# The mixer's weight parts kept in DRAM from the first token block on

## The chip, the cores and the metric

The kernel runs on one core of one Trainium2 chip. The metric is device time in microseconds for one execution. TensorE (PE) multiplies matrices out of SBUF into PSUM; VectorE (DVE) and ScalarE (ACT) do elementwise work; GpSimd (POOL) does small elementwise work and issues some of the transfers; SyncE (SP) issues most of the transfers. Each engine takes its instructions strictly in the order in which the built program has them.

## The reference, cut to what matters

One decoder layer over 2048 tokens of width 1024, in float32. A state-space branch (512 wide) and a sliding-window attention branch (512 wide) are mixed, and a gated feed-forward part follows:

```
y_ssm = glu(gelu(ssm(u)) @ w_glu + b_glu)          # w_glu: 512 x 1024
y_attn = sliding_window_attention(q, k, v, sinks)
merged = concat(rms_norm(y_ssm, g_ssm_out), rms_norm(y_attn, g_attn_out))
h = h + rms_norm(merged @ w_out, g_post_mix)       # w_out: 1024 x 1024
h = h + rms_norm(swiglu(rms_norm(h, g_pre_ffn)), g_post_ffn)
```

The change concerns `w_glu` and `w_out`. All products keep close to float32 accuracy: each operand is split into a high part (what the matmul format fp32r holds) and a low part (the rest), and three matmuls are summed: high by high, high by low, low by high (`mm3`, L216).

## The kernel before

The program has three phases. `phase_proj` computes the projections and the state-space scan and leaves them in DRAM. `phase_mix` (L692) computes the attention, the gated state-space output and the output projection, from about 340 to 800 us of the span. `phase_ffn` is the feed-forward part, until the end.

`phase_mix` goes over four blocks of 512 tokens, here called blocks 0 to 3. `dense_stream` (L930) has for each block first a **glu stage**: 8 jobs, each with one 128x512 weight tile of `w_glu` and 12 matmuls into a bank `ps_z`; after each pair of jobs ACT takes the sigmoid (`sig`, L952), DVE forms `glu` (L954), both split it into `sh` and `sl`, ACT squares it (L963) and POOL adds the squares up in `sqs`. Then come 16 **out jobs** with tiles of `w_out` into four banks `ps_wo`: 8 with the attention's operands `mah` and `mal`, then 8 with `sh` and `sl`. The sums of squares go through a small matmul (`ps_sqs`, L985). The banks of `ps_z` and `ps_wo` are the same four, so an out job's bank is free only when `glu` has read the `ps_z` in it. The attention (`attn_stream`, L760) is woven in between; its difference tile `dv` is made by POOL (L848). The row work of the block before (`post_norm`, L1009: squares on ACT, `mixr` on DVE, residual rows `res_m` loaded on SP, `hd` stored by POOL) falls into the next glu stage, and so does `channel_steps` (L1104: `hx`, `hT`, `ho`, `hb`), which prepares the feed-forward operands.

The weights of all 4 x 24 = 96 jobs come through `weights` and `fill_weights` (L889 to L912): three jobs ahead of its use, a 256 KB tile `gwr` is loaded by SP, ACT rounds it to the high part `gwh` (L170, or L173 with a gain), and DVE forms the low part `gwl` (L171 or L174). Each of the three has four buffers in the pool `g_w`, so job j needs the `gwh` and `gwl` buffers that job j-4 has used. Blocks 1 to 3 load and split the same 24 tiles again, with the same result.

The order on each engine is set when the program is built: a scheduler places instructions by priority (weights have 300 steps of precedence, L891) and by when it thinks that buffers come free.

Of the kernel before, what the change touches and what calls it, by code (L numbers as in the profile page):

```python
# [9 lines left out]
F32 = mybir.dt.float32  # L10
# [9 lines left out]
P = 128  # L20
# [23 lines left out]
def f32(ap):  # L44
    return ap.bitcast(F32)


class Layer:
# [129 lines left out]
    def setup(self):  # L178
        ctx, tc, nc, I = self.ctx, self.tc, self.nc, self.I
# [13 lines left out]
        d = self.dr  # L193
# [6 lines left out]
        self.bT_d = [[d.tile([P, 4, TB], F32, name=f"bTd_{s}_{i}") for i in range(7)] for s in range(2)]  # L200
        self.fx_d = [[d.tile([2, 7, P, TB], F32, name=f"fxd_{s}_{jp}") for jp in range(NJP)] for s in range(2)]
        self.ws_d = [[d.tile([2, P, 512], F32, name=f"wsd_{i}_{jp}") for jp in range(NJP)] for i in range(4)]
        self.cos_d = d.tile([8, SEQ], F32, name="cosd")
        self.sin_d = d.tile([8, SEQ], F32, name="sind")
        self.nsin_d = d.tile([8, SEQ], F32, name="nsind")
# [691 lines left out]
    def fill_weights(self, last):  # L897
        nc, I, gw = self.nc, self.I, self.gw
        while len(self.got) <= last:
            job = self.jobs[len(self.got)]  # L900
            n = "_".join(str(x) for x in job)
            raw = gw.tile([P, 512], F32, tag="wr", name=f"gwr_{n}")
            wh = gw.tile([P, 512], F32R, tag="wh", name=f"gwh_{n}")
            wl = gw.tile([P, 512], F32R, tag="wl", name=f"gwl_{n}")
            if job[0] == "g":
                nc.sync.dma_start(raw, I["w_glu"][job[2]])
                self.split(wh, wl, raw)
            else:
                nc.sync.dma_start(raw, I["w_out"][job[2], :, job[3] * 512:(job[3] + 1) * 512])
                c = KD + job[2]  # L910
                self.split(wh, wl, raw, self.gain[:, c:c + 1] if job[2] > 3 else None)
            self.got.append((wh, wl))  # L912

    def y_tiles(self, b):
# [625 lines left out]
```

## Time and profile before

| | before |
|---|---|
| runs | 2172.40, 2168.85, 2166.42 us; median 2168.85 |
| the profiled execution | 2164.03 us, its span 2162.3 us |
| mean granted TensorE clock | 0.975 of full speed |
| busy in the span | PE 93%, PEld (weight loads) 75%, DVE 64%, ACT 43%, POOL 14% |
| DMA | 379.7 MB, mean 176 GB/s |

Times in the traces count from the start of the span. The tables by stretch give for each engine the busy time in us and, in brackets, its instructions; then the granted TensorE clock, the mean busy share of the 16 DMA engines, and the GB/s that they moved. A number in square brackets at the end of a row is idle time of that engine just before it, with what ended it.

### The profile page before, as it was taken

The numbers are of one execution on the slowest core, as the hardware profiler recorded it, in microseconds if no ns is written. First come the engines' busy times: TensorE is split into PE (matmuls) and PEld (weight loads), VectorE is DVE, ScalarE is ACT, GpSimd is POOL, SyncE is SP. The second block draws the span as 40 slices with busy tenths as digits, with TensorE's granted clock in tenths as the row PEclk, the third lists the DMA queues.
The fourth block names the chain that finished last, engine by engine and source line by source line (L and its number), as shares of the span: only waits on it lengthen the run. The fifth ranks groups of instructions, "written<-read, shape, count | busy, mean of one in ns | idle before, by whom it ended". The sixth has DMA issues, their size and how long they took to land.

```text
span 2162.3 us, 25813 instructions
## 1 busy us (share of the span) xinstructions
PE 2012.2 (93%) x9200; PEld 1631.6 (75%) x9200; DVE 1389.5 (64%) x2199; ACT 925.1 (43%) x1468; POOL 301.7 (14%) x655
## 2 busy tenths in 40 slices
PE   7998887999999797999989998999999999999996
PEld 5777665787878675878768876887788888888885
DVE  7876888887676748556455655446766555554446
ACT  6433114976566545333323334345333333334443
POOL 3211000112223322212122110001100000000001
PEclk9999998999899998999999999999999999999998
DMA  8566657534246745657666476666523222246665
GB/s 276 213 229 191 200 148 190 144 100 158 67 148 202 270 155 178 240 138 204 208 194 155 153 264 218 199 192 231 171 102 124 95 99 105 89 165 224 204 195 185
DMA packets 177425, 379.73 MB, mean 176 GB/s; under 512 B 32864, under 2 KB 53856, under 8 KB 177104
## 3 DMA queue, kind: packets, MB, share of 16 engines
q1 hardware_dynamic: 138112, 259.89, 38.1%
q0 software_dynamic: 32512, 109.79, 15.6%
q10 hardware_dynamic: 6672, 8.40, 1.3%
q8 instruction: 72, 1.18, 0.2%
q14 instruction: 57, 0.47, 0.1%
HBM read 281.87 MB, written 119.21 MB: 185 GB/s over the span
## 4 chain that ended last, share of the span: by engine, by line
PE 42%; issue 27%; DMA 10%; DVE 7%; POOL 4%; ACT 3%; SPq 0%; DVEq 0%; POOLq 0%; ACTq 0%
PE ps_dn L221 5%; PE ps_dn L219 5%; PE ps_dn L220 5%; PE ps_gb L219 2%; PE ps_gb L221 2%; PE ps_gb L220 2%; PE ps_wo L219 2%; PE ps_wo L221 2%; PE ps_wo L220 2%; DMA hx<-hd 1%; DMA hr<-bTd 1%; DMA tab<-tabd 1%; PE ps_O L871 1%; PE ps_O L870 1%; PE ps_gc L219 1%
## 5 line engine op out<-in xcount | busy, mean ns | idle before, releaser
L219 PE MATMUL ps_gb<-bh,wh 128*128 128x512 f32 x704 | 280.3, 399 | 17.6 <-ACT wh L170 8.3
L221 PE MATMUL ps_gb<-bh,wl 128*128 128x512 f32 x704 | 275.8, 394 | 3.8 <-DVE wl L171 3.7
L220 PE MATMUL ps_gb<-bl,wh 128*128 128x512 f32 x704 | 277.7, 394 | 0.3 <-DVE bl L171 0.2
L221 PE MATMUL ps_dn<-wh_d,wl_x 128*128 128x512 f32 x616 | 241.4, 393 | 7.5 <-DVE wl_x L171 5.5
L219 PE MATMUL ps_dn<-wh_d,wh_x 128*128 128x512 f32 x616 | 241.3, 392 | 6.1 <-ACT wh_x L170 3.2
L220 PE MATMUL ps_dn<-wl_d,wh_x 128*128 128x512 f32 x616 | 240.7, 391 | 0.0
L219 PEld LDWEIGHTS ps_gb<-bh,wh 128*128 128x128 f32 x704 | 133.4, 190 | 54.3 <-ACT wh L170 10.4
L221 PEld LDWEIGHTS ps_gb<-bh,wl 128*128 128x128 f32 x704 | 133.4, 189 | 34.5 <-DVE wl L171 4.9
L220 PEld LDWEIGHTS ps_gb<-bl,wh 128*128 128x128 f32 x704 | 133.5, 190 | 29.8 <-DVE bl L171 1.5
L219 PE MATMUL ps_gc<-bh,wh 128*128 128x512 f32 x352 | 138.6, 396 | 6.9 <-ACT bh L170 6.7
L221 PEld LDWEIGHTS ps_dn<-wh_d,wl_x 128*128 128x128 f32 x616 | 115.8, 189 | 36.3 <-DVE wl_x L171 9.2
L170 ACT CAST wh<-fr 128x1024 fp32r<-128x1024 f32 (+1 forms) x88 | 73.4, 835 | 158.5 <-issue 87.4
L219 PEld LDWEIGHTS ps_dn<-wh_d,wh_x 128*128 128x128 f32 x616 | 116.3, 189 | 31.7 <-ACT wh_x L1089 4.2
L220 PE MATMUL ps_gc<-bl,wh 128*128 128x512 f32 x352 | 138.8, 395 | 0.0
L221 PE MATMUL ps_gc<-bh,wl 128*128 128x512 f32 x352 | 138.6, 394 | 0.0
L171 DVE TENSOR_TENSOR wl_x<-xr,wh_x 128x1024 fp32r<-128x1024 f32 x72 | 81.6, 1133 | 88.8 <-ACT wh_x L170 88.8
L171 DVE TENSOR_TENSOR wl_d<-dr,wh_d 128x1024 fp32r<-128x1024 f32 x84 | 95.1, 1132 | 61.5 <-ACT wh_d L170 61.5
L220 PEld LDWEIGHTS ps_dn<-wl_d,wh_x 128*128 128x128 f32 x616 | 116.3, 189 | 24.1
L170 ACT CAST wh_x<-xr 128x1024 fp32r<-128x1024 f32 x72 | 70.7, 982 | 118.9 <-PE ps_dn L220 115.6
L170 ACT CAST wh_d<-dr 128x1024 fp32r<-128x1024 f32 x84 | 82.4, 981 | 89.2 <-PE ps_dn L220 64.1
L75 DVE TENSOR_TENSOR q<-ps_ga,q 128x512 f32<-128x512 f32 x44 | 30.4, 690 | 113.7 <-PE ps_ga L221 113.2
L171 DVE TENSOR_TENSOR wl<-sb,wh 128x1024 fp32r<-128x1024 f32 x44 | 53.8, 1223 | 67.2 <-ACT wh L170 67.2
(368 smaller groups left out, 4623.1 us busy)
## 6 DMA issues: line engine op xcount, KB each, us to landing
fr<-in_w_gu SPq DMA_DIRECT2D x88, 512.0 KB
xr<-fxd SPq DMA_DIRECT2D x70, 512.0 KB
dr<-wsd SPq DMA_DIRECT2D x40, 512.0 KB
fxd<-f POOLq DMA_DIRECT2D x22, 768.0 KB, 4.3
gwr_o<-in_w_out SPq DMA_DIRECT2D x64, 256.0 KB
wsd<-in_w_down POOLq DMA_DIRECT2D x30, 512.0 KB, 10.6
dr<-in_w_down SPq DMA_DIRECT2D x30, 512.0 KB
raw<-in_xT SPq DMA_DIRECT2D x56, 256.0 KB
```

Source lines behind the costliest of these rows:

```text
L75: (eng or self.nc.vector).tensor_tensor(out=out, in0=a, in1=b, op=op)
L170: nc.scalar.copy(hi, x)
L171: nc.vector.tensor_tensor(out=lo, in0=x, in1=f32(hi), op=ALU.subtract)
L219: t.matmul(out, wh, mh, start=first, stop=False, skip_group_check=more)
L220: t.matmul(out, wh, ml, start=False, stop=False, skip_group_check=more)
L221: t.matmul(out, wl, mh, start=False, stop=last, skip_group_check=more)
L870: nc.tensor.matmul(O[:, g, :], pts[v][1][:, g, :], self.V[:, i - 1, v, :], start=True, stop=False)
L871: nc.tensor.matmul(O[:, g, :], pts[v][0][:, g, :], dv[:, v, :], start=(i == 0), stop=True)
```

## The change

Block 0 (`job[1]` is the block) loads and splits as before and then stores both parts in DRAM, one DMA of 256 KB each, issued by POOL: 48 stores. Blocks 1 to 3 load the two parts straight into `gwh` and `gwl` with two DMAs of 256 KB on SP, and have neither the raw tile nor the split: 144 loads of parts in the place of 72 raw loads, and 72 fewer splits on ACT and on DVE.

```diff
+        self.gw_d = [[d.tile([P, 512], F32, name=f"gwd_{i}_{o}") for o in "hl"] for i in range(24)]
...
             n = "_".join(str(x) for x in job)
-            raw = gw.tile([P, 512], F32, tag="wr", name=f"gwr_{n}")
             wh = gw.tile([P, 512], F32R, tag="wh", name=f"gwh_{n}")
             wl = gw.tile([P, 512], F32R, tag="wl", name=f"gwl_{n}")
+            kept = self.gw_d[len(self.got) % 24]
+            if job[1]:
+                for t, k in zip((wh, wl), kept):
+                    nc.sync.dma_start(f32(t), k)
+                self.got.append((wh, wl))
+                continue
+            raw = gw.tile([P, 512], F32, tag="wr", name=f"gwr_{n}")
             if job[0] == "g":
                 nc.sync.dma_start(raw, I["w_glu"][job[2]])
                 self.split(wh, wl, raw)
...
                 self.split(wh, wl, raw, self.gain[:, c:c + 1] if job[2] > 3 else None)
+            for t, k in zip((wh, wl), kept):
+                nc.gpsimd.dma_start(k, f32(t))
             self.got.append((wh, wl))
```

Line numbers of the changed program are higher by 1 up to the function and by 9 behind it. SP's queue in the glu stage of block 1, before: the raw loads stand together, ahead of the residual rows `res_m`.

```order
L906 DMA gwr_g_1_6_4994<-in_w_glu 128x512
L906 DMA gwr_g_1_3_5040<-in_w_glu 128x512
L906 DMA gwr_g_1_7_5085<-in_w_glu 128x512
L909 DMA gwr_o_1_4_0_5173<-in_w_out 128x512
L909 DMA gwr_o_1_5_0_5221<-in_w_out 128x512
L909 DMA gwr_o_1_6_0_5269<-in_w_out 128x512
L1029 DMA res_m0_2_5078<-in_x 128x1024
L909 DMA gwr_o_1_7_0_5326<-in_w_out 128x512
L1029 DMA res_m0_3_5147<-in_x 128x1024
```

The same place of SP's queue now.

```order
L908 DMA gwh_g_1_3_5124<-gwd_6_h_165 128x512
L908 DMA gwl_g_1_3_5125<-gwd_6_l_166 128x512
L1038 DMA res_m0_2_5160<-in_x 128x1024
L908 DMA gwh_g_1_7_5167<-gwd_7_h_167 128x512
L908 DMA gwl_g_1_7_5168<-gwd_7_l_168 128x512
L1038 DMA res_m0_3_5227<-in_x 128x1024
L908 DMA gwh_o_1_4_0_5253<-gwd_8_h_169 128x512
L908 DMA gwl_o_1_4_0_5254<-gwd_8_l_170 128x512
L1038 DMA res_m1_0_6165<-in_x 128x1024
L908 DMA gwh_o_1_5_0_5299<-gwd_9_h_171 128x512
```

The two parts of one job now stand behind a residual row of 512 KB that was loaded after them before.

POOL's queue in block 0, before: the small adds of the attention (`dv`) and of the squares (`sqs`) follow one another.

```order
L630 DMA kd_2_93<-qe_2_4_3216 2x8x512
L75 TENSOR_TENSOR dv_3_3937<-Vres_159 128x130
L75 TENSOR_TENSOR dv_4_4067<-Vres_159 128x130
L75 TENSOR_TENSOR sqs_0_3388<-sqs_0_3388,sig_0_1_3685 128x512
L75 TENSOR_TENSOR sqs_0_3388<-sqs_0_3388,sig_0_2_3861 128x512
```

The same place of POOL's queue now, from the eighteenth store on.

```order
L920 DMA gwd_8_l_170<-gwl_o_0_4_0_3907 128x512
L920 DMA gwd_9_h_171<-gwh_o_0_5_0_3984 128x512
L75 TENSOR_TENSOR dv_3_4005<-Vres_207 128x130
L920 DMA gwd_9_l_172<-gwl_o_0_5_0_3985 128x512
L920 DMA gwd_10_h_173<-gwh_o_0_6_0_4077 128x512
L75 TENSOR_TENSOR dv_4_4137<-Vres_207 128x130
L75 TENSOR_TENSOR sqs_0_3436<-sqs_0_3436,sig_0_1_3747 128x512
L920 DMA gwd_11_h_175<-gwh_o_0_7_0_4236 128x512
```

Nineteen stores have come in front of `dv_3`, and `dv_4` stands behind the store of the high part of out job 6.

PE at the end of block 1's glu stage, before: the third and fourth bank (`ps_wo_559`, `ps_wo_560`) come late, and products of the next weight tiles are drawn forward.

```order
L221 MATMUL ps_wo_558_5323<-gwh_o_1_4_0_5174,mal_5_4483 128x512
L219 MATMUL ps_wo_557_5322<-gwh_o_1_5_0_5222,mah_4_4301 128x512
L220 MATMUL ps_wo_557_5322<-gwl_o_1_5_0_5223,mah_4_4301 128x512
L221 MATMUL ps_wo_557_5322<-gwh_o_1_5_0_5222,mal_4_4302 128x512
L219 MATMUL ps_wo_559_5324<-gwh_o_1_4_0_5174,mah_6_4834 128x512
```

The same place of PE's queue now.

```order
L222 MATMUL ps_wo_558_5397<-gwh_o_1_4_0_5253,mal_5_4567 128x512
L220 MATMUL ps_wo_559_5398<-gwh_o_1_4_0_5253,mah_6_4924 128x512
L221 MATMUL ps_wo_559_5398<-gwl_o_1_4_0_5254,mah_6_4924 128x512
L222 MATMUL ps_wo_559_5398<-gwh_o_1_4_0_5253,mal_6_4925 128x512
L220 MATMUL ps_wo_560_5399<-gwh_o_1_4_0_5253,mah_7_5156 128x512
```

The first weight tile is now used for all four banks before the second.

## Rows read from the trace of the kernel before

**Rows 1.** The page's first part, PE: busy us, share of the span, instructions.

```profile
PE 2012.2 (93%) x9200; PEld 1631.6 (75%) x9200; DVE 1389.5 (64%) x2199; ACT 925.1 (43%) x1468; POOL 301.7 (14%) x655
```

**Rows 2.** The table by stretch: from and to, length, then PE, PEld, DVE, ACT, POOL busy us with their instructions, granted clock, DMA share, GB/s.

```profile
515.00:525.00 10.00, 9.81 (x44) 7.80 (x43) 8.32 (x10) 5.43 (x10) 2.42 (x8) 1.00 0.40 117
525.00:535.00 10.00, 7.00 (x30) 5.12 (x28) 10.00 (x11) 8.69 (x15) 3.32 (x3) 1.00 0.94 352
535.00:545.00 10.00, 6.18 (x19) 4.66 (x19) 6.78 (x8) 5.99 (x9) 8.79 (x18) 0.83 0.87 264
545.00:555.00 10.00, 9.52 (x47) 9.52 (x47) 3.31 (x9) 1.96 (x5) 0.84 (x2) 0.54 0.12 29
555.00:565.00 10.00, 10.00 (x55) 9.06 (x56) 6.68 (x15) 4.81 (x11) 0.00 (x0) 0.77 0.26 80
...
640.00:650.00 10.00, 6.70 (x37) 5.16 (x36) 10.00 (x11) 8.92 (x13) 6.36 (x8) 1.00 0.97 339
...
710.00:720.00 10.00, 9.55 (x40) 7.52 (x39) 7.43 (x11) 3.33 (x4) 2.13 (x3) 0.84 0.98 343
720.00:730.00 10.00, 8.87 (x40) 7.03 (x39) 7.56 (x13) 6.05 (x10) 2.86 (x4) 1.00 0.98 336
...
760.00:770.00 10.00, 8.48 (x41) 6.66 (x40) 7.94 (x10) 7.95 (x13) 5.99 (x16) 1.00 0.99 373
```

**Rows 3.** PE's timeline in blocks 1 to 3, all rows from 524 to 800 us before which it waited more than 0.9 us except one at 648 us and one at 661 us, and the two rows that bound a pair of glu jobs: start us, us, engine, line, what, and the idle time before.

```profile
523.89 0.50 PE L219 MATMUL ps_z<-yh,gwh_g 128*128 128x512 f32 x1 [0.18 <-ACT sig L952]
...
529.50 0.39 PE L219 MATMUL ps_wo<-gwh_o,mah 128*128 128x512 f32 x1
...
531.89 0.50 PE L219 MATMUL ps_wo<-gwh_o,mah 128*128 128x512 f32 x1 [1.55 <-DVE glu L954]
535.38 0.60 PE L219 MATMUL ps_wo<-gwh_o,mah 128*128 128x512 f32 x1 [1.83 <-ACT sig L952]
545.48 0.38 PE L985 MATMUL ps_sqs<-ones,sqs 128*128 128x1 f32 x2 [3.92 <-POOL sqs L75]
...
643.39 0.50 PE L219 MATMUL ps_wo<-gwh_o,mah 128*128 128x512 f32 x1 [1.55 <-DVE glu L954]
...
708.18 0.79 PE L219 MATMUL ps_wo<-gwh_o,sh 128*128 128x512 f32 x1 [4.81 <-DVE mixr L997]
727.10 0.47 PE L219 MATMUL ps_z<-yh,gwh_g 128*128 128x512 f32 x1 [1.13 <-ACT wh L170]
733.81 1.97 PE L1125 MATMUL ps_hT<-ident,hx 128*128 128x128 f32 x8 [3.03 <-ACT hx L1117]
753.68 0.50 PE L219 MATMUL ps_wo<-gwh_o,mah 128*128 128x512 f32 x1 [0.92 <-DVE glu L954]
756.14 0.50 PE L219 MATMUL ps_wo<-gwh_o,mah 128*128 128x512 f32 x1 [1.48 <-ACT sig L952]
762.27 0.50 PE L219 MATMUL ps_wo<-gwh_o,mah 128*128 128x512 f32 x1 [1.52 <-DVE glu L954]
```

**Rows 4.** DVE's timeline around the end of block 1's glu stage, in the same columns.

```profile
524.54 0.74 DVE L174 SCALAR_TENSOR_TENSOR gwl_o<-gwr_o,c_gains,gwh_o 128x512 fp32r<-128x512 f32 x1
...
528.19 1.79 DVE L174 SCALAR_TENSOR_TENSOR gwl_o<-gwr_o,c_gains,gwh_o 128x512 fp32r<-128x512 f32 x1
...
531.10 0.74 DVE L954 SCALAR_TENSOR_TENSOR glu<-ps_z,l_b_glu,sig 128x512 f32<-128x512 f32 x1
531.76 0.74 DVE L174 SCALAR_TENSOR_TENSOR gwl_o<-gwr_o,c_gains,gwh_o 128x512 fp32r<-128x512 f32 x1
...
534.54 0.74 DVE L174 SCALAR_TENSOR_TENSOR gwl_o<-gwr_o,c_gains,gwh_o 128x512 fp32r<-128x512 f32 x1
...
537.84 0.74 DVE L954 SCALAR_TENSOR_TENSOR glu<-ps_z,l_b_glu,sig 128x512 f32<-128x512 f32 x1
```

**Rows 5.** The weight tiles by instruction over the whole span: line, engine, operation, what, count, then ns at least, in the median and at most, first and last start in us.

```profile
L909 SPq DMA_DIRECT2D gwr_o<-in_w_out x64: 327/328/570, 374.8 to 781.7; - x64
L173 ACT ACTIVATE gwh_o<-gwr_o,c_gains x32: 704/716/759, 384.2 to 768.9; 128x512 fp32r<-128x512 f32 x32
L174 DVE SCALAR_TENSOR_TENSOR gwl_o<-gwr_o,c_gains,gwh_o x32: 720/744/2125, 386.5 to 769.6; 128x512 fp32r<-128x512 f32 x32
L170 ACT CAST gwh_o<-gwr_o x32: 602/621/642, 448.5 to 791.2; 128x512 fp32r<-128x512 f32 x32
L171 DVE TENSOR_TENSOR gwl_o<-gwr_o,gwh_o x32: 680/692/693, 449.1 to 791.9; 128x512 fp32r<-128x512 f32 x32
...
L170 ACT CAST gwh_g<-gwr_g x32: 602/620/624, 352.5 to 741.0; 128x512 fp32r<-128x512 f32 x32
L171 DVE TENSOR_TENSOR gwl_g<-gwr_g,gwh_g x32: 680/690/694, 353.2 to 745.1; 128x512 fp32r<-128x512 f32 x32
```

**Rows 6.** Transfers: from the chain of work in order of time the time of one raw weight load (start us, us); from POOL's timeline the issue of a 512 KB store; and from the instructions on `mixr` between 500 and 560 us the time from issue to landing of four such stores.

```profile
344.31 3.75 DMA gwr_g<-in_w_glu
...
521.86 0.62 POOL L1033 DMA_DIRECT2D hd<-mixr  x1 [5.21 <-DVE mixr L75]
...
DMA to landing us min/median/max: 4.7/5.9/7.4
```

**Rows 7.** Block 0: a `dv` on POOL, and on DVE the first weight split behind it.

```profile
406.19 0.42 POOL L75 TENSOR_TENSOR dv<-Vres 128x130 f32<-128x130 f32 x1 [12.64 <-PE ps_O L871]
...
410.42 0.74 DVE L174 SCALAR_TENSOR_TENSOR gwl_o<-gwr_o,c_gains,gwh_o 128x512 fp32r<-128x512 f32 x1
```

## The prediction, made blind

> **What bounds the kernel now.** I read the page's first part, then the table by stretch, then TensorE's timeline for every wait in blocks 1 to 3, and last the weight tiles by instruction. PE is busy for 93% of the span, DVE for 64%, ACT for 43% [rows 1]. So work taken from DVE or ACT is worth only what PE waited for it, and what PE's clock lost behind such waits. The reader is to see in [rows 3] that these waits sit where a glu stage hands over to the out jobs, and in [rows 2] that DVE is there busy for 10.00 of 10 us (525 to 535, 640 to 650) while the DMA engines too are near their limit: a mean busy share of 0.94 to 0.99 at 336 to 373 GB/s. The change takes work from the first of these two resources and puts more on the second. That is the whole question.
>
> **What is removed.** Each of 72 jobs loses an ACT instruction of 0.62 or 0.72 us and a DVE instruction of 0.69 or 0.74 us [rows 5]: with the medians 24 glu jobs, 24 out jobs with a gain and 24 without give 47 us of ACT and 51 us of DVE. Most of it lies beside PE's work and is worth nothing there. It counts in these places.
>
> Block 1's change-over. PE waits 1.55 us for `glu`, 1.83 for `sig` and 3.92 at `ps_sqs` for the sum of squares that POOL forms from what `sig` and `glu` led to: 7.30 us [rows 3]. In that time DVE has no idle time, and four weight splits (0.74 + 1.79 + 0.74 + 0.74 = 4.0 us) stand before the last `glu` at 537.84 [rows 4]. Without them that `glu` starts about 4 us earlier; ACT's splits go as well. Of 7.30 us I leave about 2, for the residual rows' work, which stays: a gain of 5.3. At most all 7.3 go, at least nothing, if `glu` then waits for something else.
>
> The clock behind it. In the three stretches from 535 to 565 the granted clock is 0.83, 0.54 and 0.77, after 1.00 before the waits [rows 2], and PE is busy for 9.52 and 10.00 us in the last two, so the time there is the clock's. The loss is 10 x (0.17 + 0.46 + 0.23) = 8.6 us. The 0.54 is about the lower of the two levels, 1.2 of 2.4 GHz. If PE's gap shrinks from 7.3 to 2 us the clock may hold or may still fall; bounds 0 and 8.6, and I take the half, 4.3, since a wait of 1.55 us at 643 left the clock at 1.00 in its stretch, while one of 4.81 at 708 stands ahead of a stretch at 0.84 [rows 2, 3].
>
> Blocks 2 and 3. Block 2 has a wait of 1.55 us for `glu`; the share kept in block 1 (5.3 of 7.3, 0.73) gives 1.1. Block 3 has 0.92, 1.48 and 1.52 us for `glu` and `sig`, and 1.13 us directly for ACT's high part of a glu weight: 5.05 us in all, of which the same share is 3.7 [rows 3]. The waits for `mixr` (4.81) and `hx` (3.03) come from row work that stays: 0, at best the 4.81 too.
>
> **What is added to the transfers.** A job of blocks 1 to 3 now loads 512 KB instead of 256. Two glu jobs take 529.50 - 523.89 = 5.6 us on PE, one 2.8 [rows 3], so weights alone ask for 0.524 MB / 2.8 us = 187 GB/s where it was 94. Averaged over the span there is room. In the saturated stretches (525 to 535, 640 to 650, 710 to 730, 760 to 770 in [rows 2], 50 us) there is none. I count 14 jobs there, fewer than 50 / 2.8 = 18 because PE waits in them: 14 x 0.262 = 3.7 MB more, at 0.35 MB per us (their mean) 10.5 us. Loads are issued three jobs ahead, 3 x 2.8 = 8.4 us; of this a raw load of 3.75 us alone, and 4.7 to 7.4 us for a transfer of 512 KB among others [rows 6], leave about 4. So I let half of the 10.5 reach PE: a loss of 5.3, with bounds 0 and 10.5 from this term by bandwidth alone.
>
> The Trainium skill, "DMA: Bandwidth & Descriptors" (Measured; Where 436 GB/s comes from), gives 425 GB/s for a large read on one core whose neighbour is idle, and about 358 per core when both read. By the first the 3.7 MB would take 8.7 us and by the second 10.3 (an estimate from that page), so the loss would be 4.4 or 5.2 in the place of 5.3; the trace's fullest stretch has 373 GB/s at a share of 0.99 and so stands by the second.
>
> The queue. SP takes 0.33 us per issue [rows 5], and 144 issues replace 72, 24 us more in blocks 1 to 3: no limit by itself. But the raw tile gave the load four buffers of its own, free as soon as a split had read it; now a load may start only when PE has done with job j-4, and both loads of a job stand in line behind the residual rows, which wait for DVE's `mixr` adds. With four buffers the period of a job is max(11.2, L + 2.8) / 4 us, where L is the time from a buffer's freeing to the landing of both parts. L up to 8.4 us costs nothing. 512 KB landed in 4.7, 5.9 (median) and 7.4 us [rows 6], so it just fits; if SP is held for 2 us in addition, it does not. In the sum this is 0, and the price of the last rival.
>
> **Block 0's stores.** POOL issues 48 stores, 0.62 us each by a 512 KB store in its queue [rows 6]: 30 us of a POOL that is busy 14% [rows 1]. Nineteen come in front of `dv_3`, and `dv_4` stands behind one whose weight split is the row at 410.42, where a `dv` of the attention ran at 406.19 [rows 7]. So `dv` may be up to 4.2 us later, and who waits for it is the attention, not at once PE, which has products of out jobs beside it. I take 0; bounds 0 and 4. No stall of the buffers: four of them, and a store needs 4.7 to 7.4 us, about what two or three jobs take.
>
> **The sum**, against the profiled execution (2164.03 us: a span of 2162.3 and 1.7 around it): -5.3 - 4.3 - 1.1 - 3.7 + 5.3 + 0 + 0 = -9.1, so 2155. The median of the runs is 4.8 above that execution; for a median I forecast 2168.85 - 9.1 = 2160.
>
> **Rivals.** *The waits vanish wholly.* If the last `glu` no longer binds, 7.3 + 8.6 + 1.55 + 5.05 = 22.5 us go and some 2.5 come from DMA: -20, 2149. For it speaks that four splits are more than either single wait for `glu` or `sig`; against it the saturated transfers in the same stretches.
>
> *A transfer takes the place of the split.* PE then waits for weights where it waited for `glu`: -14.4 of gains and up to 10.5 + 2 of losses, -2, 2167. For it: DVE's busiest stretches are DMA's too [rows 2]. Against it: the first out jobs' weights come three jobs early.
>
> *Stores that cannot start.* If a POOL store could not be issued while DVE works, each of the 24 pairs would be held by half a DVE instruction or so, 24 x 0.35 = 8 us of later buffers in block 0, which use up the gain: -1, 2168. Against it: the issue of `hd` took 0.62 us, and four such stores landed within 7.4 us [rows 6], from stretches in which DVE was busy for 8.32 and 10.00 of 10 us [rows 2]. The Trainium skill, "SBUF — State Buffer" (SBUF: two separate sides), has such a rule: a DMA issued by GpSimd waits while DVE runs an operation that takes both of its ports.
>
> *Slower: weights late on SP.* Both parts stand in SP's order behind residual rows and `hx` work, with only four buffers. From L above 8.4 us each job loses (L - 8.4) / 4; with L = 10.4, that is a landing of 7.4 us and 3 us of SP waiting, 0.5 us on each of the 40 jobs that lie in or beside the row work of blocks 1 to 3 is +20, and the DVE and clock gain of about 10 stays: +10, 2179. For it: the order on SP, where a job's loads now stand behind a row of 512 KB that was loaded after them. Against it: the median landing of 5.9.
>
> **How the numbers follow.** Forecast 0.33 (own range 2154 to 2164), vanishing waits 0.17, transfer in their place 0.26, held stores 0.04, late weights 0.20. The extremes by the bounds are 7.3 + 8.6 + 1.55 + 5.05 + 4.81 = -27 (2142) and 10.5 + 4 = +15 without a gain (2184). The range of 8 in 10 is 2142 to 2182. A change of 0.3%, 6.5 us (2162.3 to 2175.4), is about what a measurement can tell from none. Faster: 0.33 x 0.85 + 0.17 + a little of the third, 0.46; same: the rest of these, the third and fourth, and a tenth of the last, 0.35; slower: 0.19.
>
> **What would show it.** Right: DVE busy below 9 in 525 to 535; no PE wait over 1 us at `ps_sqs` in block 1; a clock above 0.9 in most of 535 to 565; PE waits named for `gwh` or `gwl` loads under 0.5 us on average, with L under 8.4. Wrong: PE rows in blocks 1 to 3 ended by DMA of several us each, the more of them in the stretches with a DMA share over 0.95; or `dv` waits in block 0; or the same gap at `ps_sqs`, ended by another producer, with the same fall of the clock.

## The result, and the profile after

| | before | changed |
|---|---|---|
| first measurement, 4 runs each | median 2168.68 us | median 2179.49 us, ratio 1.0051, 95% interval 1.0031 to 1.0072 |
| second, 35 and 12 runs | median 2174.28 us | median 2179.81 us, ratio 1.0021, 95% interval 1.0001 to 1.0040 |
| the profiled execution (span) | 2162.3 us | 2176.2 us |
| mean granted TensorE clock | 0.975 | 0.969 |
| DMA | 379.7 MB | 411.2 MB |

The kernel is slower, by 0.2 to 0.5%; the lower end of the second interval all but touches no change. The page's first part of the changed kernel against [rows 1]: DVE has lost 47 us of work and ACT 41 (51 and 47 had been worked out), and PE, which does the same products, is busy for 10 us more.

```profile
PE 2022.5 (93%) x9200; PEld 1640.7 (75%) x9200; DVE 1342.6 (62%) x2127; ACT 883.9 (41%) x1396; POOL 318.5 (15%) x703
```

To find where, I cut PE's timeline at the first product of each block's glu stage and at the first of the feed-forward part. First the kernel before, then the changed one.

```profile
356.88 2.07 PE L219 MATMUL ps_z<-yh,gwh_g 128*128 128x512 f32 x4 [0.54 <-ACT yh L170]
...
507.22 0.39 PE L219 MATMUL ps_z<-yh,gwh_g 128*128 128x512 f32 x1
...
618.44 0.39 PE L219 MATMUL ps_z<-yh,gwh_g 128*128 128x512 f32 x1
...
723.08 0.39 PE L219 MATMUL ps_z<-yh,gwh_g 128*128 128x512 f32 x1
...
802.05 0.39 PE L219 MATMUL ps_gb<-bh,wh 128*128 128x512 f32 x1
```

```profile
359.57 0.79 PE L220 MATMUL ps_z<-yh,gwh_g 128*128 128x512 f32 x1 [0.48 <-ACT yh L170]
...
513.60 0.39 PE L220 MATMUL ps_z<-yh,gwh_g 128*128 128x512 f32 x1
...
618.01 0.39 PE L220 MATMUL ps_z<-yh,gwh_g 128*128 128x512 f32 x1
...
726.21 0.39 PE L220 MATMUL ps_z<-yh,gwh_g 128*128 128x512 f32 x1
...
811.63 0.39 PE L220 MATMUL ps_gb<-bh,wh 128*128 128x512 f32 x1
```

The differences give block 0 154.0 us in the place of 150.3 (+3.7), block 1 104.4 for 111.2 (-6.8), block 2 108.2 for 104.6 (+3.6), block 3 85.4 for 79.0 (+6.5): 452.1 for 445.2, +6.9. A second profile of the changed kernel gave 154.8, 103.1, 109.0 and 84.1, +5.8. Of the 13.9 us between the two spans of the table, 2.7 lie ahead of block 0 and 4.3 behind block 3, in stretches that hold the same instructions in both kernels. In the nineteen profiles of this document the stretch ahead ended anywhere from 356.9 to 368.2 us and the one behind took 1360.1 to 1365.8, so a whole time says little here.

A block's length says more, but not always to a few tenths of a microsecond. The kernel before and one whose blocks 1 to 3 have the same order on PE, DVE, ACT and SP ("stores only" below) agree within 0.2 us in each of these blocks. Profiles with the changed kernel's order there ("changed", "changed, again" and "one pair stored"; for blocks 1 and 2 also "rs_sd on DVE") lie further apart: 102.9 to 104.4, 108.2 to 112.1 and 83.4 to 85.4 us. A difference of 1 or 2 us against one of them is not shown by a single profile.

The table by stretch of the changed kernel, to be held against [rows 2], and behind it two rows of the kernel before that [rows 2] leaves out. Block 1 starts 6.4 us later here than before, block 2 0.4 us earlier and block 3 3.1 later.

```profile
525.00:535.00 10.00, 10.00 (x46) 8.29 (x45) 7.74 (x10) 6.77 (x12) 3.00 (x4) 1.00 0.88 302
535.00:545.00 10.00, 6.96 (x19) 4.46 (x18) 5.85 (x7) 6.08 (x9) 7.15 (x18) 0.67 1.05 401
545.00:555.00 10.00, 10.00 (x75) 9.42 (x74) 5.07 (x12) 4.75 (x10) 1.50 (x2) 0.98 0.62 165
...
640.00:650.00 10.00, 5.42 (x26) 5.42 (x27) 4.90 (x9) 6.73 (x11) 7.11 (x18) 0.72 1.06 395
650.00:660.00 10.00, 10.00 (x47) 8.85 (x47) 4.24 (x8) 4.94 (x7) 2.77 (x3) 0.77 0.66 184
...
770.00:780.00 10.00, 4.50 (x18) 3.40 (x17) 1.25 (x1) 3.29 (x6) 5.17 (x19) 0.87 0.60 201
```

```profile
650.00:660.00 10.00, 9.39 (x63) 8.02 (x62) 7.04 (x13) 6.04 (x11) 5.83 (x16) 1.00 0.66 178
...
770.00:780.00 10.00, 9.68 (x43) 7.69 (x42) 2.45 (x4) 4.24 (x7) 3.72 (x18) 1.00 0.34 116
```

In block 1 (first three rows) DVE falls from 10.00 to 7.74 of 10 us in 525 to 535. The clock over 535 to 565 is 0.67, 0.98 and (by the same table) 1.00, where it was 0.83, 0.54 and 0.77. In block 2 PE falls to 5.42 us in 640 to 650 and the clock to 0.72 and 0.77, where it was 1.00. In block 3 PE has 4.50 us of work in 770 to 780, where it had 9.68. PE's timeline names what it waited for in these places (as [rows 3]).

```profile
536.82 0.47 PE L220 MATMUL ps_wo<-gwh_o,mah 128*128 128x512 f32 x1 [1.30 <-DMA gwh_o<-gwd_h]
537.81 0.50 PE L221 MATMUL ps_wo<-gwl_o,mah 128*128 128x512 f32 x1 [0.52 <-DMA gwl_o<-gwd_l]
...
540.99 0.80 PE L220 MATMUL ps_wo<-gwh_o,mah 128*128 128x512 f32 x1 [1.22 <-ACT sig L961]
...
644.59 0.69 PE L1134 MATMUL ps_hT<-ident,hx 128*128 128x128 f32 x2 [4.66 <-ACT hx L1126]
...
778.77 0.80 PE L220 MATMUL ps_wo<-gwh_o,mah 128*128 128x512 f32 x1 [5.50 <-ACT mixr L1003]
```

The 7.30 us of waits in block 1 have become 3.04. The new ones are 4.66 us for `hx` in block 2 (1.76 before, at the row at 648 us that [rows 3] leave out) and 5.50 us for ACT's `mixr` in block 3, both row work. The wait for DVE's `mixr` at the end of block 2, 4.81 us before, is longer too: 5.50 here, and 6.32, 7.22 and 6.19 in the other three profiles of this order. DVE's `mixr` stands there behind an operation on `ho` that waits for the landing of a store `bTd` (operands of the feed-forward part, issued by POOL), 1.63 us before and 5.80 now. PE's row now, and DVE's row of `ho` before and now:

```profile
712.80 0.79 PE L220 MATMUL ps_wo<-gwh_o,sh 128*128 128x512 f32 x1 [5.50 <-DVE mixr L1006]
```

```profile
706.17 1.29 DVE L75 TENSOR_TENSOR ho<-ps_hT,c_gains 128x512 f32<-128x512 f32 x2 [1.63 <-DMA bTd<-ho]
```

```profile
710.80 1.29 DVE L75 TENSOR_TENSOR ho<-ps_hT,c_gains 128x512 f32<-128x512 f32 x2 [5.80 <-DMA bTd<-ho]
```

Weights are waited for 1.82 us in all of blocks 1 to 3, at the first out job of block 1 alone (the first two rows of PE's timeline above). Its loads in SP's timeline:

```profile
527.46 0.72 SPq L908 DMA_DIRECT2D gwh_o<-gwd_h  x1
528.27 0.72 SPq L908 DMA_DIRECT2D gwl_o<-gwd_l  x1
```

From issue to the product that waited for it the high part took 9.4 us (527.46 to 536.82), in stretches with a DMA share of 0.88 and 1.05.

### The profile page after: what moved, and what is told of

Read it like the earlier page. It is cut to its first block, busy times and chain, and to the rows that moved or that the text cites. A ratio compares the mean times of both kernels' runs of the same rounds, so it can differ in the third digit from the quotient of the medians.

```text
span 2176.2 us, 25807 instructions
## 1 busy us (share of the span) xinstructions
PE 2022.5 (93%) x9200; PEld 1640.7 (75%) x9200; DVE 1342.6 (62%) x2127; ACT 883.9 (41%) x1396; POOL 318.5 (15%) x703
## 4 chain that ended last, share of the span: by engine, by line
PE 42%; issue 27%; DMA 10%; DVE 7%; POOL 4%; ACT 3%; SPq 0%; DVEq 0%; POOLq 0%; ACTq 0%
PE ps_dn L222 5%; PE ps_dn L221 5%; PE ps_dn L220 5%; PE ps_gb L220 2%; PE ps_gb L222 2%; PE ps_gb L221 2%; PE ps_wo L220 2%; PE ps_wo L221 2%; PE ps_wo L222 2%; DMA hr<-bTd 1%; PE ps_O L872 1%; PE ps_O L871 1%; DMA hx<-hd 1%; PE ps_gc L220 1%; PE ps_gc L222 1%
## 5 line engine op out<-in xcount | busy, mean ns | idle before, releaser
L170 ACT CAST wh<-fr 128x1024 fp32r<-128x1024 f32 (+1 forms) x88 | 73.5, 836 | 160.3 <-issue 86.8
```

The costliest lines, as they stand in the source:

```text
L170: nc.scalar.copy(hi, x)
```

## The experiments

The table has the length of each block in us, from PE's timeline as above, and the ratio of the time to that of the kernel before, with its interval. The runs are told behind it in the order of the questions.

| kernel | block 0 | 1 | 2 | 3 | sum | ratio |
|---|---|---|---|---|---|---|
| before | 150.3 | 111.2 | 104.6 | 79.0 | 445.2 | 1 |
| changed | 154.0 | 104.4 | 108.2 | 85.4 | 452.1 | 1.0051 (1.0031 to 1.0072) |
| changed, again | 154.8 | 103.1 | 109.0 | 84.1 | 451.0 | 1.0021 (1.0001 to 1.0040) |
| stores only | 153.8 | 111.2 | 104.4 | 79.1 | 448.6 | 1.0005 (0.9988 to 1.0022) |
| one pair stored | 151.1 | 103.0 | 112.1 | 83.4 | 449.6 | 1.0002 (0.9987 to 1.0016) |
| high part only | 154.2 | 100.9 | 108.7 | 80.4 | 444.2 | 0.9979 (0.9965 to 0.9992) |
| before, more bytes | 151.2 | 115.2 | 104.2 | 79.0 | 449.6 | 1.0024 (1.0003 to 1.0044) |
| five buffers | 149.1 | 104.6 | 109.5 | 82.9 | 446.1 | 1.0013 (0.9993 to 1.0032) |
| rows loaded by ACT | 157.5 | 109.3 | 109.1 | 82.5 | 458.4 | 1.0051 (1.0031 to 1.0071) |
| hT later | 154.2 | 103.1 | 112.0 | 86.8 | 456.0 | 1.0019 (0.9996 to 1.0041) |
| hT later, hx on POOL | 151.2 | 102.8 | 106.2 | 82.9 | 443.2 | 1.0016 (0.9997 to 1.0034) |
| rows first | 153.5 | 102.8 | 109.4 | 78.3 | 444.0 | 1.0008 (0.9984 to 1.0031) |
| the last two together | 154.6 | 102.5 | 105.8 | 78.4 | 441.3 | 0.9994 (0.9973 to 1.0015) |
| rs_sd on DVE | 152.0 | 102.9 | 111.5 | 80.6 | 447.1 | 1.0003 (0.9985 to 1.0022) |
| out jobs only | 150.8 | 104.6 | 120.1 | 78.1 | 453.6 | 1.0013 (0.9992 to 1.0035) |
| out jobs only, hT later | 151.1 | 105.4 | 116.1 | 77.0 | 449.5 | 0.9997 (0.9975 to 1.0020) |
| block 1's out jobs only | 151.0 | 104.3 | 107.7 | 79.4 | 442.4 | 0.9975 (0.9956 to 0.9995) |
| blocks 1 and 3, out jobs | 150.9 | 104.0 | 108.5 | 86.8 | 450.1 | 1.0009 (0.9991 to 1.0028) |
| together, glu parts stored in block 1 | 150.6 | 108.4 | 110.3 | 78.1 | 447.3 | 1.0011 (0.9990 to 1.0031) |

**Is it the stores or the read-back?** Stores alone, with blocks 1 to 3 as before (`job[1]` is never above 3):

```diff
-            if job[1]:
+            if job[1] > 9:
...
-            for t, k in zip((wh, wl), kept):
+            for t, k in zip((wh, wl), kept) if not job[1] else ():
                 nc.gpsimd.dma_start(k, f32(t))
```

> Block 0 stores both parts by POOL as in the change; blocks 1 to 3 load and split the raw tiles as before, so that only POOL's order differs from the kernel before. Theory A (two causes: the stores crowd the transfers of block 0's glu stage, +4.6 us between the first and the last product of that stage in the changed kernel's trace; the read-back costs the rest): 2173, with the DMA share of 350 to 375 us near 0.98 as in the changed kernel and a lower clock there. Rival B (the whole loss is the read-back's): 2169. Rival C (the whole loss is the stores'): 2179.

And the read-back with 2 stores in the place of 48:

```diff
-            kept = self.gw_d[len(self.got) % 24]
+            kept = self.gw_d[0]
...
-            for t, k in zip((wh, wl), kept):
+            for t, k in zip((wh, wl), kept) if not self.got else ():
```

> Only the parts of the first weight tile are stored (2 stores in the place of 48), and all 144 loads of blocks 1 to 3 read that one pair, so the products of blocks 1 to 3 are those of one tile. The orders of PE, DVE, ACT and SP are the changed kernel's. Theory A: block 0 takes what it took before, and blocks 1 to 3 still gain about 7 us in block 1 and lose about 10 in blocks 2 and 3: 2173 to 2175. Rival B (the read-back alone): 2179. Rival C (the stores alone): 2165, below the kernel before.

Each costs its own part, as theory A has it: block 0 153.8 with all stores and 151.1 with two; blocks 1 to 3 294.7 with the splits of before (294.8) and 298.5 with the read-back (changed: 298.0 and 296.2). The times are 1.0005 and 1.0002: an effect of 3.5 us is inside an interval of 0.17%, so by time alone both would have been called free. That they lie at theory A's 2173 is luck, as the kernel before took 2174.2 us beside them. What the stores do is in ACT's timeline of block 0, first before, then with the stores alone.

```profile
360.52 2.42 ACT L800 CAST QS<-qraw 128x512 fp32r<-128x512 f32 x4 [3.69 <-DMA qraw<-qd]
```

```profile
364.69 1.14 ACT L801 CAST QS<-qraw 128x512 fp32r<-128x512 f32 x2 [5.14 <-DMA qraw<-qd]
366.94 1.14 ACT L801 CAST QS<-qraw 128x512 fp32r<-128x512 f32 x2 [1.11 <-DMA qraw<-qd]
```

The stores of the first four glu jobs are issued from 356 to 361 us, and the attention's query rows, loaded in that time, come later. The table by stretch has it too, if both stretches are laid from 5 us ahead of the block's first product (356.88 and 359.60) to 10 us behind it; before, and with the stores alone:

```profile
351.88:366.88 15.00, 10.53 (x35) 7.49 (x35) 10.90 (x18) 9.10 (x14) 0.00 (x0) 0.68 0.80 177
```

```profile
354.60:369.60 15.00, 8.99 (x25) 6.06 (x24) 8.69 (x15) 7.96 (x13) 4.38 (x8) 0.73 1.08 295
```

The DMA share goes from 0.80 to 1.08, and PE does 8.99 us of work in the place of 10.53. (The expectation's stretch, 350 to 375, has 0.81 and 0.95, but it holds 2.7 us less of the block in the second kernel.) Over the block's first 25 us the clock is 0.76 in the place of 0.91. That the stores hold the weight buffers is not the reason: PE waits for no weight part in block 0 of this run. With no store of glu weights, or of one pair, block 0 took 150.3 to 151.2 us in eight profiles; with all 48 stores and the changed kernel's queues and buffers it took 153.5 to 154.8 in seven, 151.2 and 152.0 in two more. So the cost is 1 to 4 us, mostly 3.5. In the two that were spared, the block's first product had itself waited 4.01 and 2.96 us for `yh` (1.1 us or less in the seven), so the query rows had more time ahead of the cut; that this is why is not shown. The two kernels left out here have another order in block 0: with five buffers four products for the queries stand ahead of the cut, so that its 149.1 us can't be compared.

**The changed kernel once more.**

> The changed kernel once more, for its time in more runs and for a second profile. From the first profiles: from the first product of block 0's glu stage to the first of the feed-forward part it took 452.1 us against 445.2 before (+6.9), the stretch before it and the stretch behind it hold the same instructions in both. Theory A (stores +3.5 in block 0, read-back +3.2 in blocks 1 to 3, added up): a ratio of 1.003, 7 us. Rival E (the two alone cost nothing by their times, 1.0005 and 1.0002, and the first four runs were by chance high): 1.001. By blocks theory A wants 154, 104, 108 and 85 us again, within 1.5 each.

1.0021 lies nearer to rival E's 1.001 than the first measurement, its blocks are theory A's. I take the blocks.

**Bytes or order?** Half the bytes with the change's order: blocks 1 to 3 read the high part alone and use it as the low part too.

```diff
-                for t, k in zip((wh, wl), kept):
-                    nc.sync.dma_start(f32(t), k)
-                self.got.append((wh, wl))
+                nc.sync.dma_start(f32(wh), kept[0])
+                self.got.append((wh, wh))
```

> Blocks 1 to 3 read back the high part alone and use it in the place of the low part too, so a job loads 256 KB as in the kernel before and has no split; the block 0 of the changed kernel, its stores too, is kept, and on PE, ACT and DVE nearly its order. Theory D (bytes: the second 256 KB of each job crowd the loads of hx and of the residual rows): block 2 takes 103 to 105 and block 3 78 to 80 us, as before or less, the waits for hx and mixr shrink. Theory O (order: the engines' order that follows from the absent splits exposes hx and mixr, whatever the bytes): block 2 stays at 108 to 109 and block 3 at 84 to 85. Block 0 154 and block 1 103 to 105 in both.

And the order of before with the change's bytes:

```diff
             raw = gw.tile([P, 512], F32, tag="wr", name=f"gwr_{n}")
+            if job[1]:
+                more = gw.tile([P, 512], F32, tag="wm", name=f"gwm_{n}", bufs=2)
+                nc.sync.dma_start(more, I["w_glu"][len(self.got) % 8])
```

> The kernel before, with its splits and nearly its order, but each job of blocks 1 to 3 also loads a second tile of 256 KB that nothing uses; no stores. It has the changed kernel's bytes without its order. Theory D (bytes): blocks 1 to 3 get longer by what the changed kernel lost there, block 2 108 or more and block 3 83 or more, with the waits for hx and mixr longer; the time 7 us or more above before. Theory O (order): 111, 105 and 79 us as before, the time within 2 us of before.

Theory D falls for block 2: 108.7 with half the bytes, 104.2 with twice the bytes and the order of before. For block 3 both gave little (80.4 and 79.0), so neither bytes nor the absent splits alone are its cause, and theory O, which wanted 84 to 85 with half the bytes, falls there. Bytes have a price in block 1, +4.0, where PE's timeline of this kernel shows the old wait for `glu` grown from 1.55 us (and the one for `sqs` from 3.92 to 4.43):

```profile
543.23 0.79 PE L219 MATMUL ps_wo<-gwh_o,mah 128*128 128x512 f32 x1 [5.35 <-DVE glu L957]
```

Against the profiles of the changed kernel's order, half the bytes gave back 2.0 to 3.5 us in block 1 and 3.0 to 5.0 in block 3. But SP has half as many loads of parts in that run, and POOL's order has moved with them, so it does not part bytes from order.

**Block 2.** On PE the first `hT` of the changed kernel stands directly behind the glu stage; before, 16 products stood between. So it was moved back:

```diff
+            if i == 0:
+                with self.tc.high_priority(-30):
+                    return turned(x, i)
+            return turned(x, i)
```

> The changed kernel with the first two transposes of hx in block 2 given a priority 30 steps lower: on PE 24 products of the first two out jobs now stand ahead of the first hT, where none did (16 in the kernel before); hardly anything else moves. Theory P for block 2 (PE's order, not the transfers: hT stands first behind the glu stage and PE waits 4.66 us for hx with products at hand, then the clock is at half for 10.2 us): the wait at hT is under 1.5 us, the clock holds, block 2 takes 103 to 105 us in the place of 108.2, the whole 4 us less than the changed kernel. Rival D (the loads of 512 KB per job hold hx back): hT and hx are late as before or later, block 2 takes 108 or more.

Theory P fell. Of the 24 products ahead of `hT` six ran, from 637.71 us on; then the wait came back in full, now for `sig`:

```profile
644.61 0.80 PE L220 MATMUL ps_wo<-gwh_o,mah 128*128 128x512 f32 x1 [4.46 <-ACT sig L961]
```

That led to ACT's timeline, here of the changed kernel.

```profile
643.38 1.15 ACT L1126 ACTIVATE hx<-hx,rstd 128x1024 f32<-128x1024 f32 x1 [1.49 <-issue]
644.44 2.04 ACT L170 CAST yh<-yraw 128x512 fp32r<-128x512 f32 x2
646.37 0.69 ACT L961 ACTIVATE sig<-ps_z,l_b_glu 128x512 f32<-128x512 f32 x1
```

PE ended the glu stage at 639.9, but the last `sig` runs at 646.37, behind an `hx` and two `yh`; what this `hx` waited for in the 1.49 us ahead of it the profile does not name ("issue"). Before, `sig` stood behind `hx` too; there PE had the 16 products on the other banks. The next run keeps the later `hT` and gives that one `hx` to POOL; PE, DVE and SP have the same order in both.

```diff
+            if i == 0:
+                nc.gpsimd.tensor_scalar(out=got[i], in0=got[i], scalar1=self.rstd2[:, i:i + 1], scalar2=None, op0=ALU.mult, op1=ALU.bypass)
+                return
```

> As the run with the first hT behind 24 products (where the wait of 4.5 us in block 2 came back as one for ACT's sig), and the first hx of block 2 is scaled by POOL in the place of ACT; everything else as there. Theory Q for block 2 (ACT's order: the last sig stands behind an hx that waits for its load and behind two yh, 6.4 us after PE has ended the glu stage): sig no longer waits for hx, PE's wait at the first out products of block 2 falls from 4.5 us to under 2.5, block 2 takes 103 to 106 us. Rival D (the yh in between wait for yraw loads, which are as late as hx): sig is as late, PE waits 4 us or more, block 2 takes 108 or more.

Theory Q holds in so far as ACT's order goes: PE's wait of 4.46 us at this place is 1.90, and block 2 takes 106.2 us in the place of 112.0.

```profile
648.65 0.50 PE L220 MATMUL ps_wo<-gwh_o,mah 128*128 128x512 f32 x1 [1.90 <-ACT sig L961]
```

In the run with both cures below, block 2 takes 105.8 us. There `sig` follows the two `yh` on ACT at 641.96, and PE waits 0.88 us:

```profile
641.96 0.69 ACT L961 ACTIVATE sig<-ps_z,l_b_glu 128x512 f32<-128x512 f32 x1
```

```profile
642.70 0.50 PE L220 MATMUL ps_wo<-gwh_o,mah 128*128 128x512 f32 x1 [0.88 <-ACT sig L961]
```

ACT's order is not all of block 2. The two runs in which block 1 reads back and block 2 loads and splits as before (told last) have in block 2 the order of before on every engine, and still take 107.7 and 108.5 us there, where three profiles of that order behind an unchanged block 1, or nearly that order, took 104.2 to 104.6. In the first of them DVE's `ho` waits 4.70 us for the landing of a store `bTd` (2.94 before), and PE 2.31 us for that `ho`.

```profile
667.61 0.69 DVE L75 TENSOR_TENSOR ho<-ps_hT,c_gains 128x512 f32<-128x512 f32 x1 [4.70 <-DMA bTd<-ho]
```

So in these two runs part of block 1's gain comes back as a loss in block 2 with no change of order there. That the shorter block 1 is the reason is not shown, and why these stores land later is open.

**Block 3.** The chain of the changed kernel, followed back from PE's 5.50 us: ACT's `mixr` waits 5.43 us for the landing of an `hd` store (a buffer of `mixr`), POOL issues this store at 771.08, DVE has added the row's residual at 766.63 after waiting for its load, and SP issues that load at 761.04, behind two weight parts for whose buffers it had waited since 756.5. One fence for each engine's timeline: ACT, POOL, DVE, SP.

```profile
778.03 0.69 ACT L1003 ACTIVATE mixr<-ps_wo,rs_a 128x512 f32<-128x512 f32 x1 [5.43 <-DMA hd<-mixr]
```

```profile
771.08 0.60 POOL L1042 DMA_DIRECT2D hd<-mixr  x1 [0.26 <-issue]
```

```profile
766.63 1.23 DVE L75 TENSOR_TENSOR mixr<-mixr,res_m 128x1024 f32<-128x1024 f32 x1 [1.21 <-DMA res_m<-in_x]
```

```profile
755.65 0.83 SPq L908 DMA_DIRECT2D gwl_o<-gwd_l  x1
760.12 0.32 SPq L908 DMA_DIRECT2D gwh_o<-gwd_h  x1
760.49 0.46 SPq L908 DMA_DIRECT2D gwl_o<-gwd_l  x1
761.04 0.52 SPq L1038 DMA_DIRECT2D res_m<-in_x  x1
```

Three runs take the load out of its place on SP: five buffers for each part (and two for the raw tile), the rows' loads issued by ACT, and the rows' loads 500 steps up in priority.

```diff
-            wh = gw.tile([P, 512], F32R, tag="wh", name=f"gwh_{n}")
+            wh = gw.tile([P, 512], F32R, tag="wh", name=f"gwh_{n}", bufs=5)
```

> The changed kernel with five buffers for each part and two for the raw tile, the same memory. Theory A for block 3 (the last residual row stands on SP behind loads that wait until PE has freed a buffer, its hd store comes late, and ACT and PE wait 5.5 us for it): a load can go one job, 2.8 us, earlier, most of the wait of 5.5 us at 779 us and the clock behind it are gone, 2173. Rival D (the transfers' bandwidth is what is short in blocks 2 and 3): as many bytes in the same time, 2179 or above.

```diff
-            nc.sync.dma_start(x, src(t))
+            (nc.scalar if follow else nc.sync).dma_start(x, src(t))
```

> The changed kernel with the residual rows' loads issued by ACT in the place of SP. Theory A for block 3: the last row no longer stands behind weight loads, the PE wait for ACT's mixr shrinks from 5.5 us to under 1, 2173. Rival D (bandwidth): the row lands as late as before, 2179. It may also cost: ACT's own work stands behind a load that waits for its buffer, then sig waits on PE grow, 2182.

```diff
-            nc.sync.dma_start(x, src(t))
+            with self.tc.high_priority(500 if follow else 0):
+                nc.sync.dma_start(x, src(t))
```

> The changed kernel with the residual rows' loads 500 steps up in priority: on SP the last one of block 3 now stands ahead of the parts of out jobs 6, 7 and 4_1, where it stood behind them; else nearly the changed kernel's order. Theory S for block 3 (SP's order): the row lands earlier, ACT's mixr and with it PE no longer wait 4.5 to 5.5 us, block 3 takes 80 to 82 us in the place of 84 to 85. Rival D (bytes) or T (weights are now late in its place): 84 or more, with PE waiting for gwh or gwl loads.

Five buffers brought block 3 to 82.9 with the wait still 3.77 us. Loading by ACT ended the wait for `mixr` (82.5), but it cost 3.5 us in block 0 (157.5) and 5 in block 1 (109.3). Rows first gave 78.3, all of block 3's loss. But in the last two the scheduler had also moved POOL's `hd` store. In the seven profiles until then with a PE wait of over 3 us for `mixr`, this store stands on POOL behind operations of the chain that makes `rs_sd`; in those without the wait it stands ahead of them. POOL's order before, and in the changed kernel (13 rows of the chain left out):

```
L1033 DMA hd_101<-mixr_1_6473 128x1024
L1033 DMA hd_101<-mixr_2_6474 128x1024
L1033 DMA hd_101<-mixr_3_6475 128x1024
L75 TENSOR_TENSOR sqs_7202<-sqs_7202,sig_3_7485 128x512
```

```
L1042 DMA hd_101<-mixr_2_6500 128x1024
L87 TENSOR_SCALAR rsq_vd_7544<-ssq_sd_7541 128x4
...
L99 TENSOR_TENSOR rs_sd_7542<-rsq_td_7546,rsq_yd_7547 128x4
L1042 DMA hd_101<-mixr_3_6501 128x1024
```

In the changed kernel's trace the sum is ready at 767.9 (766.63 + 1.23) and the store issued at 771.08. One more run therefore moves that chain to DVE; the order of PE, ACT and SP stays as it is, row for row.

```diff
-                            self.rsqrt(rs_s, ssq, SSMW, 4)
+                            self.rsqrt(rs_s, ssq, SSMW, 4, eng=nc.vector if b == 3 else None)
```

> The changed kernel with one thing moved: the fifteen small operations on POOL that make rs_sd in block 3, which stand there ahead of the last hd store, are done on DVE. The orders of PE, ACT and SP are the changed kernel's, row for row. Theory V (POOL's order): the residual row's sum is ready at 767.9 us in the changed kernel's trace and the hd store is issued at 771.1; without the operations it is issued at once, 3 us earlier, so PE's wait for ACT's mixr falls from 4.5 to 5.5 us to 1.5 to 2.5, block 3 takes 80 to 82 us in the place of 84 to 85. Theory S (SP's order: the row's load stands behind weight parts that wait for PE): SP's order is the same, so the wait is 4.5 us or more and block 3 takes 84 to 85 again.

POOL's and PE's timelines of that run:

```profile
774.99 0.55 POOL L1042 DMA_DIRECT2D hd<-mixr  x1 [5.03 <-DVE mixr L75]
```

```profile
781.19 0.50 PE L220 MATMUL ps_wo<-gwh_o,mah 128*128 128x512 f32 x1 [2.13 <-ACT mixr L1003]
```

The store goes as soon as the sum is there, the wait is 2.13 us (3.37 to 5.50 in the three profiles with the chain on POOL) and block 3 80.6. So POOL's order is worth 2.8 to 4.8 us of block 3's loss: theory V for the larger part. The rest, 1.6 us against the kernel before, may be the place of the load on SP (theory S); no run moved that load alone.

**The cures together, and smaller versions.**

> The two together. If Q and S hold, block 2 takes 104 and block 3 81 us, the whole phase 443 us with block 0's 154: 2 us below before and 7 below the changed kernel; the stores' 3.5 us in block 0 stay. If Q and S don't hold, 450 as the changed kernel.

The phase takes 441.3 us, 10.8 below the changed kernel and 3.9 below before, with the stores of block 0 still in it. By its time, 0.9994, it can't be told from before. Storing the glu parts in block 1 did not help (the conditions on top of the three cures):

```diff
-            if job[1]:
+            if job[1] > (job[0] == "g"):
...
-            for t, k in zip((wh, wl), kept):
+            for t, k in zip((wh, wl), kept) if job[1] == (job[0] == "g") else ():
```

> The last kernel (hx on POOL, hT behind 24 products, residual rows first) with the glu weights' parts stored in block 1 in the place of block 0: block 0 stores the 32 parts of the out jobs alone, block 1 splits its glu weights once more, blocks 2 and 3 read everything back. If the three causes are the right ones and independent: block 0 151 us as in the runs with out jobs alone, block 1 103 to 105, block 2 106, block 3 78: 439 in the place of 445.2 before and 452.1 changed, a ratio to before of 0.997. If the stores only move their cost into block 1, that block takes 107 or more and the whole 442 to 443, within 0.2% of before.

Against the run with the cures alone, block 0 gave 4.0 us back and block 1 took 5.8, block 2 4.5. Keeping the out jobs alone, without and with the later `hT`:

```diff
-            if job[1]:
+            if job[1] and job[0] == "o":
...
-            for t, k in zip((wh, wl), kept):
+            for t, k in zip((wh, wl), kept) if not job[1] and job[0] == "o" else ():
```

> Only the 16 out jobs of a block are stored and read back; the 8 glu jobs load and split in every block as before. Theory A: the 16 stores that met the attention's and the scan's loads in block 0's glu stage are gone, so block 0 takes 150 to 152 us (before 150.4, changed 154.0); block 1 keeps its gain, since the four splits ahead of its last glu were of out weights, 104 to 106; blocks 2 and 3 between before and changed, 106 and 82. Together 2 to 4 us below the kernel before. Rival D (bandwidth): blocks 2 and 3 as the changed kernel, 108 and 85, no gain over before.

> The last two together: out jobs alone kept, and the first hT of block 2 behind 24 products. If both theories hold, about 150, 105, 103 and 82 us: 5 us below the kernel before, a ratio of 0.998. If only the order of PE or only the stores matter, it is the same as before within 0.1%.

Blocks 0 and 1 came as expected, block 3 better (78.1 and 77.0), block 2 did not (120.1 and 116.1); why was not followed up. Last, the read-back where it was seen to help, in block 1, and in blocks 1 and 3 (`job[1] == 1` and `job[1] in (1, 3)` in the condition above):

> Only block 1 reads back, and only its 16 out jobs; blocks 2 and 3 load and split as before, and block 0 stores 32 parts. From the profiles so far: block 0 150.8 (the run with out jobs alone), block 1 104.6, blocks 2 and 3 as before, 104.6 and 79: 439 us where the kernel before takes 445, 6 us below it, a ratio of 0.997. If the gain of block 1 is only moved (the row work behind it comes back in block 2), block 2 takes 108 or more and nothing is gained.

> The out jobs of blocks 1 and 3 read back, block 2 as before: as the last one, with block 3 at 77 to 78 us by the two runs with out jobs alone: 438 us, 7 below the kernel before, a ratio of 0.997. If the bytes in block 3's saturated stretches matter, block 3 takes 82 or more.

Block 1's out jobs alone are the one version with all its products that beats the kernel before by its time: 0.9975, 0.9956 to 0.9995, median 2169.52 against 2174.55 us. Its blocks give 2.8 of these 5.0 us, and it is one of eighteen intervals, so some of it may be chance. The expectation had 439 us and got 442.4, as block 2 took 3 us more than before, though nothing was changed in it. With block 3 in it the wait for `mixr` is back (3.85 us) and nothing is left.

## Why the prediction was wrong

The time lies in the range that I gave, and the sign of the forecast is wrong: -9 us forecast, +5.5 and +10.8 measured by the medians.

*Block 1's change-over and the clock behind it* came out near in size. The waits went from 7.30 to 3.04 us (-4.3, forecast -5.3), and the wait at `ps_sqs` is gone. The clock's loss over 535 to 565 us went from 8.6 to 3.5 by the prediction's own sum (-5.1, forecast -4.3). The block gained 6.8 and 8.1 us where -5.3 - 4.3 and a share of the transfers' +5.3 had been put down. The mechanism was right for `glu`, not in full for `ps_sqs`: before, ACT had the last square at 540.1 us and POOL added it at 544.17, behind the fifteen small operations of `rstd` that end the row work. So those 3.92 us hung on the row work, of which the forecast said that it stays; in the changed kernel that chain starts 23.8 us into the block in the place of 30.7 (POOL's timelines, 537.35 and 537.94 us). The signs that were to show the forecast right came true, all but L; those with a place in the trace were all in block 1.

*Blocks 2 and 3* are the failed step: "The waits for mixr (4.81) and hx (3.03) come from row work that stays: 0". The work stays, but its place does not. Without the splits the scheduler put `hT` ahead of the out products and left PE nothing to do behind ACT's late `sig` (block 2), and it put a residual row's load behind weight parts on SP and its `hd` store behind fifteen small operations on POOL (block 3). And a wait that was to stay as it was grew: the 4.81 us became 5.50 to 7.22, behind a store that lands later. Two runs lost 3.1 and 3.9 us in block 2 with its old order. Forecast -1.1 and -3.7, measured +3.6 and +6.5 (+4.4 and +5.1 in the second profile). What the runs show in its place: ACT's order is a cause of block 2's loss and POOL's of most of block 3's; that stores landing later add to block 2 is seen in the waits, and why they land later stays open. I had read SP's, POOL's and PE's order for the places in blocks 0 and 1 alone; the same listing of blocks 2 and 3 had the moves in it.

*The transfers* (+5.3). The extra bytes cost 4.0 us in block 1 with the order of before, and nothing in blocks 2 and 3. With the changed order up to 5.0 us of block 3 go with half the bytes, but through an order that moved too. So the size was near, and its place can't be told.

The fullest stretch that I had read, 373 GB/s at a share of 0.99, is not the trace's fullest: the kernel before itself moved 392 GB/s at 1.03 in 50 to 60 us, and the changed one 401 in 535 to 545. The prediction had weighed two figures of the Trainium skill, "DMA: Bandwidth & Descriptors" (Measured): 425 GB/s for a core alone and about 358 where both cores of a pair stream. I had put the trace by the second; both 392 and 401 lie above it, and 401 is nearer the first.

*The queue* (0) and the rival built on it. The rival's time, 2179, came out and its cause did not: with L at 9.4 us or more in one place, above the 8.4 from which it was to decide, PE waited 1.82 us for weights in all. That the time fits is luck. What was late was the row work behind them.

*Block 0's stores* (0, at most +4) cost 1 to 4 us, mostly 3.5, but not through `dv` on POOL. The work that I took to hide them was the wrong one: the attention's query loads come in the 15 us around the block's start, where the stores took the DMA share from 0.80 to 1.08. That stretch was not among the rows that I had read.

*Held stores* did not show: the issue of a store by POOL took 0.53 to 0.61 us throughout.

## What to carry to other kernels

When a change takes work out of a kernel whose order a scheduler makes, compare the whole order, engine by engine, for what has moved ahead of a wait or behind a long chain, and not only at the place of the change. Where whole times cannot tell 4 us apart, cutting the profile at fixed products and comparing the stretches often can; take the same kernel twice to see how far a stretch repeats (here 0.2 us in one order and up to 3.9 in another), and lay stretches from the same product and not from the same time. A cure of one wait can come back as another further on: look at the blocks behind it, too. Stores that run beside other work want their price read from the transfers under way in their very stretch.

## What was not expected of the hardware

Two things. The DMA share of a 10 us stretch goes above 1, before and after: the kernel before moved 392 GB/s at a share of 1.03 where I had read no rows, the changed one 401 at 1.05.

```profile
50.00:60.00 10.00, 10.00 (x44) 7.90 (x43) 4.32 (x6) 3.63 (x8) 5.47 (x18) 1.00 1.03 392
```

And the stretch ahead of the change, with the same instructions, varied by 11 us between executions.
